# mLSTM pairs with two sum tiles and their own order, weight preparation placed behind the HGRN level copies, Silu written as Sigmoid and a product

## The chip, the cores and the metric

The kernel runs on one core of a Trainium2 chip. The metric is the device time of one execution in microseconds (us). A core has five engines, each with its own in-order queue: TensorE (PE, matmuls; PEld is the load of its weights, which runs beside it), VectorE (DVE), ScalarE (ACT), GpSimd (POOL) and SyncE (SP), which here only issues DMAs.

## What is computed

One step of a hybrid streaming encoder for 512 prompt frames and 32 sample frames (544 columns), all in float32 with a width of 1024. One wide projection feeds two branches: four mLSTM heads (matrix memory, width 512 a head) and eight HGRN2 heads (gated linear attention, width 128 a head). Two sigmoid gates merge the branches, and an output product and a gated per-layer embedding follow.

```python
xn = _rmsnorm(h, norm_g[l])
proj = xn @ w_in[l]
u, v_m, z_m, ig_pre, fg_pre, q_h, f_h, i_h, g_h, ga, gb = jnp.split(proj, ...)
c, conv_new = _causal_conv(u, conv0[l], conv_w[l], conv_b[l])
c = jax.nn.silu(c)
qm = einsum('bthd,hde->bhte', ch, w_qm[l])
km = einsum('bthd,hde->bhte', ch, w_km[l]) * (M_HD ** -0.5)
hm, C_new, n_new, m_new = _mlstm(qm, km, vm, ig, lf, C0, n0, m0)
hm = (_head_layernorm(hm, mnorm_g[l]) + m_skip[l] * c) * jax.nn.silu(z_m)
ya = hm @ w_brm[l]
lfh = jnp.log(lb + (1.0 - lb) * jax.nn.sigmoid(f_lin))
kh = (1.0 - lb) * jax.nn.sigmoid(-f_lin)
qh = jax.nn.silu(q_h)
oh, S_new = _hgrn(qh, kh, i_h, lfh, S0)
oh = _head_rmsnorm(oh, hnorm_g[l]) * jax.nn.silu(g_h)
yb = oh @ w_brh[l]
y = jax.nn.sigmoid(ga) * ya + jax.nn.sigmoid(gb) * yb
h = h + y @ w_out[l]
h = h + jax.nn.sigmoid(h @ w_pg[l]) * (p[l] @ w_ple[l])
out = _rmsnorm(h, final_g)
```

## The kernel before

**Precision.** A float32 operand is split in two parts, a high one (`...h`, a cast, mostly by ACT) and the low rest (`...l`, a subtraction, mostly by DVE). A product is three matmuls (high·high, low·high, high·low) that accumulate in PSUM. All 544 columns go in two halves of 272, each in its own PSUM half; a tile d, q, k, ya or yb is such a pair of halves.

**Pairs.** The projection `proj` is computed two units of 128 rows at a time. A `Two` takes units a and b and saves one product in eight by Strassen's scheme, in seven blocks of 12 matmuls: `a11`, `a12` and `a22` use a raw piece of the weights; `s1`, `s2`, `s3` and `s4` use sums of raw pieces. `form` makes the sums in the tiles `ws` (pool tag `wu`, `NSUM` of them) and splits them into `wsNh` and `wsNl` (`waNNh`, `waNNl` for raw pieces; the number behind is the unit: ws26 is the s2 of unit 6). The sums s1, s2 and s4 are made one over the other in one tile: s2 adds to s1, s4 adds to s2. `s3`, `s2` and `a22` write the same PSUM half, and between them ACT copies that half out (`t`, line 490), so a block in that half waits for the copy of the one before.

**Two kinds of pairs.** In the HGRN part and at the end pairs are `early` (the raw pieces are summed by accumulating DMAs that POOL issues, line 451 among them) or `apart` (the first of them, unit 48, which stands in the last mLSTM head). The mLSTM pairs (u, v and z) are neither, and their sums are DVE additions.

**The pump.** `Pump` lines the blocks of all pairs up in one order by the numbers in `PAIR`, and hands them out a half block at a time as filling between matmuls of the recurrences that wait for ACT and DVE. The order on PE is written by hand (`manual_schedule`). The orders on ACT and DVE come from a scheduler that takes instructions by readiness and priority; `high_priority` puts an instruction ahead, `issue_after(x)` keeps it from standing before x on x's engine. `pump.behind` is such an x for all weight preparations.

**The order of the work.** A first stretch (to about 60 us) takes the norm and the u pairs. Then four mLSTM heads: products k and q, scores (`sc`, line 844), `kt`, `vt` and `C`, then `nm` and `Cs`, then the transposes `yt`, then `ya`. In the first head the gate rows (lines 690 to 715, the generator `gates`) stand on DVE too: additions and scans over a 4 x 544 tile. The copies `z<-d` (line 653) empty the PSUM halves which k then takes. From 627 us eight HGRN heads of about 33.5 us each run: in each, seven levels (`LEVELS`) in which ACT copies `km` (line 1471), PE makes `pl` from it (line 1479), and DVE multiplies and selects (lines 1501, 1508). ACT makes the gates of the next head with Sigmoid (1388, 1389), its query with Silu (1397, 1398), and its output gate with Silu (1419). Then two sets of transposes `ht` (1546, copied to `kit` by ACT in 1550) and the state's product `su`. From about 935 us the last pairs (ga and gb, the merge gates) are computed, then `yb`, `o`, `pg` and the rest. The embedding p comes in by DMA as tiles p (line 1645) and is split to ps0 and ps1; `pleo` (line 1654) empties its product.

Of the kernel before, what the change touches and what calls it, by code (L numbers as in the profile page):

```python
# [14 lines left out]
ALU = mybir.AluOpType  # L15
# [27 lines left out]
NSUM = 4  # L43
# [10 lines left out]
GATED = 2  # L54
# [10 lines left out]
def hybrid_step(ctx: ExitStack, tc: tile.TileContext, a, o):  # L65
# [320 lines left out]
    class Two:  # L386
# [7 lines left out]

        def raws(self):
            a, b = self.unit, self.other
            return [(a, 0), (a, 1)] + ([] if self.early else [(b, 0)]) + [(b, 1)]
# [27 lines left out]
        def make(self, *forms):  # L425
            def go(raw):
                for form in forms:
                    if form not in self.w:
                        self.form(form, raw)

            return go

        def form(self, form, raw):
# [14 lines left out]
            src = raw[plain_[form]] if form in plain_ else q["s3" if form == "s3" else "s1"]  # L448
            self.w[form] = split_piece(src, f"w{form}{a}")
# [89 lines left out]
    ALONE, PAIR = (0, 1, 2, 3), (0, 1, 5, 4, 6, 9, 10)  # L539

    class Pump:


        def __init__(self, todo):
            self.done, self.when, self.behind, self.limit = 0, {}, None, None
            order, base = [], 0
            for n, e in enumerate(todo):
                if isinstance(e, One):
# [7 lines left out]
            self.begins = [(first.index((n, 0)) - LEAD, e) for n, e in enumerate(todo) if isinstance(e, Two) and e.early]  # L556
            self.order = [b for *_, b in sorted(order, key=lambda x: x[:3])]
# [7 lines left out]
        def prepare(self, upto):  # L565
            while self.made < min(upto, self.limit or len(self.order)):
# [72 lines left out]
    def fill(h):  # L639
# [9 lines left out]
        def gate_one(f, acc):  # L649
            z = eslot(f"z{h}{f}")  # L650
            for b in range(2):
                with tc.high_priority():
                    V.tensor_copy(z[:, b * TH : (b + 1) * TH], acc[b][:, :TH])
# [153 lines left out]
    def stage_q(h, u):  # L807
# [4 lines left out]
        w = t.pop("wq", None) or weight(a["w_qm"][h, u], f"wq{h}{u}")  # L812
# [89 lines left out]
    def mchain(h, pump):  # L902
# [76 lines left out]
        yield pump.clear(4)  # L979
# [188 lines left out]
    with tc.manual_schedule(engines={mybir.EngineType.Activation, mybir.EngineType.DVE, mybir.EngineType.PE}):  # L1168
# [145 lines left out]
        for _ in range(GATED):  # L1314
            next(gates)
    with tc.manual_schedule(engines={mybir.EngineType.PE}):
        for h in range(MH):
            if h:
                stage_decay(h)
            else:  # L1320
                st8[0].update(vt=vt, cc=cc, cs=cs)
                pump.to(EARLY)
            stage_k(h)
# [17 lines left out]
            if h == 0:  # L1341
                with tc.issue_after(low.ins):
# [29 lines left out]
    gbs, yas = [None] * KD, [None] * KD  # L1372

    def units():
# [19 lines left out]
        def query(h, qq):  # L1394
            tf, kk, kq = (hs[h][k] for k in ("tf", "kk", "kq"))
            q0 = eslot(f"q0{h}")
            S.activation(unrev(q0), qq[:, :HB], AF.Silu)
            S.activation(q0[:, HB:T], qq[:, HB:T], AF.Silu)
# [15 lines left out]
        def gate(h, t):  # L1414
            S.activation(t[:, :T], t[:, :T], AF.Silu)
            hs[h]["gg"] = t

        def merge_a(f, t):
# [3 lines left out]
            V.tensor_tensor(y, y, t[:, :T], ALU.mult)  # L1422
# [33 lines left out]
    def chain(h):  # L1456
# [9 lines left out]
        for li, c in enumerate(LEVELS):  # L1466
            smp = c < NS
            n = HB if smp else NA
            km = tp.tile([P, NA], F32, tag="vs", name=f"km{h}{c}", bufs=1)
            with tc.high_priority():  # L1470
                S.copy(  # L1471
                    km.rearrange("p (n j c) -> p n j c", j=2, c=c),
                    view(kk, HB, ((2 * c, NA // (2 * c)), (c - HB, 2), (1, c))),
                )
            yield STEPS[li]
# [66 lines left out]
        for n, src, dst, dss in ((0, ii, it, its), (1, kk, kt, kts)):  # L1542
# [15 lines left out]
        yield 3  # L1558
# [66 lines left out]
    obf = []  # L1625
# [17 lines left out]
    for k in range(2):  # L1643
        t = slot(f"p{k}")
        nc.sync.dma_start(t[:, :T], a["pT"][k])
        ps_.append(split(t[:, :T], f"ps{k}"))

    def ple_units(n):
        for f in range(len(ple), len(ple) + n):
# [3 lines left out]
            for b in range(2):  # L1653
                S.copy(t[:, half(b)], acc[b])
# [177 lines left out]
```

## Time and profile before

| quantity | value |
|---|---|
| median of 3 runs | 1186.71 us (1183.53 to 1187.61) |
| profiled execution | 1184.37 us |
| its span | 1182.7 us |
| POOL busy | 186.7 us (16%) |
| DMA moved | 159.93 MB, mean 135 GB/s |

The span is the part of the execution between the first and the last recorded instruction; 1.7 us of the profiled execution lie outside. An engine is busy when an instruction of it runs. A wait is put down to the instruction that ended it. A row of the timeline gives start, duration, engine, line, what is written and what is read; in square brackets at its end stands how long the engine had been idle and what it waited for. Line numbers are those of the kernel before, in the changed kernel they lie up to some 30 lines further on.

### The profile page before, as it was taken

The page shows a single profiled execution, that of the slowest core. Times are in us where ns is not written, and L with a number is a line of the kernel's source. Part 1 is how long each engine was busy: PE and PEld are TensorE (multiplying, and loading weights), DVE is VectorE, ACT ScalarE, POOL GpSimd, SP SyncE. Part 2 cuts the span into 40 slices and gives each one's busy share as a digit, 9 for nine tenths or more (in the row PEclk, how much of TensorE's full clock was granted, in tenths as well). Part 3 has the DMA queues.
Part 4 walks back from the last instruction along what each step waited for, and adds up shares of the span by engine and source line. Part 5 has one row for each costly group of instructions (what it writes and reads, how often), then busy time and mean ns, then how long its engine had stood idle before and what let it go on. Part 6 is the DMA issues. An engine that isn't in the chain of part 4 may idle for free.

```text
span 1182.7 us, 24120 instructions
## 1 busy us (share of the span) xinstructions
PE 1146.8 (97%) x8897; PEld 1117.9 (95%) x8897; DVE 885.4 (75%) x1975; ACT 701.1 (59%) x1521; POOL 186.7 (16%) x364
## 2 busy tenths in 40 slices
PE   9989999999999999999999999999999989999998
PEld 8989999999999999899989999999999989999998
DVE  6976988576886777976885688888888755654485
ACT  5666656656556565565654577777776655432462
POOL 4933010100001100001100122322222220000000
PEclk9999999999999999999999999999999989999999
DMA  6224215322353223542738666655666685432653
GB/s 227 64 90 129 75 46 163 119 95 95 126 168 127 90 91 128 156 158 78 229 101 261 159 137 135 135 126 127 133 155 131 165 226 130 147 95 81 232 170 112
DMA packets 91150, 159.93 MB, mean 135 GB/s; under 512 B 10260, under 2 KB 17812, under 8 KB 91032
## 3 DMA queue, kind: packets, MB, share of 16 engines
q1 hardware_dynamic: 80928, 140.24, 37.2%
q0 software_dynamic: 9936, 18.09, 9.6%
q8 instruction: 70, 1.15, 0.4%
q14 instruction: 48, 0.39, 0.1%
q10 hardware_dynamic: 168, 0.06, 0.0%
HBM read 133.44 MB, written 24.91 MB: 134 GB/s over the span
## 4 chain that ended last, share of the span: by engine, by line
PE 80%; DVE 9%; ACT 5%; DMA 4%; issue 3%; SPq 0%; POOL 0%; ACTq 0%; DVEq 0%; POOLq 0%
PE d L476 31%; PE ya L151 8%; PE pg L1691 4%; PE yb L151 4%; PE o L151 4%; PE k L151 4%; PE q L151 4%; PE C L884 4%; PE pl L1479 2%; PE nm L1058 2%; PE sc L844 2%; DMA ws<-in_w_in 2%; PE d L369 1%; DVE cv L618 1%; PE ple L151 1%
## 5 line engine op out<-in xcount | busy, mean ns | idle before, releaser
L405 POOL DMA_DIRECT2D ws<-in_w_in x46 | 40.4, 877 | 163.5 <-DMA ws<-in_w_in 36.8
L490 ACT COPY t<-d 128x272 f32<-128x272 f32 x126 | 47.4, 378 | 19.3 <-PE d L476 16.9
L1501 DVE TENSOR_TENSOR hkq<-hkq,q 128x288 f32<-128x288 f32 (+1 forms) x96 | 40.8, 432 | 16.3 <-PE pl L1479 12.6
L1479 PE MATMUL pl<-hkq,km 128*128 128x128 f32 x224 | 39.4, 298 | 4.5 <-ACT km L1471 4.4
L618 DVE SCALAR_TENSOR_TENSOR cv<-ub,vec,cv 128x547 f32<-128x547 f32 x48 | 40.3, 842 | 1.9 <-ACT cv L613 1.5
L1479 PEld LDWEIGHTS pl<-hkq,km 128*128 128x128 f32 x224 | 30.9, 189 | 7.7 <-ACT km L1471 6.4
L1471 ACT COPY km<-hkq 128x256 f32<-128x256 f32 x56 | 23.9, 427 | 16.2 <-PE d L476 12.3
L451 POOL DMA_DIRECT2D ws<-in_w_in x23 | 23.7, 1031 | 60.6 <-DVE ws272l L131 26.1
L988 DVE SCALAR_TENSOR_TENSOR c<-c,wi,Cs 128x258 f32<-128x258 f32 x32 | 15.1, 478 | 17.0 <-PE Cs L986 16.9
L1452 POOL TENSOR_SCALAR_AFFINE_SELECT aa<-at 128x128 f32<-128x128 f32 x32 | 20.7, 678 | 43.1 <-DVE at L1508 38.4
L1126 DVE TENSOR_TENSOR y<-ya,y 128x272 f32<-128x272 f32 x48 | 19.2, 436 | 9.9 <-PE ya L151 8.7
L1508 DVE COPY_PREDICATED at<-lmask,pl 128x288 f32<-128x288 uint8 (+1 forms) x56 | 26.3, 470 | 0.0
L896 ACT COPY Co<-C 128x258 f32<-128x258 f32 x32 | 10.4, 378 | 25.2 <-PE C L884 11.0
L782 POOL COPY vsm<-vt 128x96 f32<-128x96 f32 x16 | 6.4, 408 | 91.5 <-DVE vt L497 54.7
L1069 ACT COPY y<-nm 128x516 f32<-128x516 f32 x16 | 9.4, 589 | 17.6 <-PE nm L1058 17.5
L1598 ACT ACTIVATE osq<-kq 128x128 f32<-128x128 f32 x32 | 9.8, 305 | 15.2 <-DVE kq L1592 15.0
L858 ACT CAST sh<-dm 128x512 fp32r<-128x512 f32 (+3 forms) x16 | 7.4, 460 | 19.1 <-DVE dm L852 19.1
L1018 DVE BATCH_NORM_STATS2 bs<-y 128x6 f32<-128x512 f32 (+1 forms) x20 | 13.8, 691 | 6.1 <-ACT y L1069 6.0
L1058 PE MATMUL nm<-vhl,sh 128*128 128x258 f32 x112 | 18.3, 286 | 0.0
L960 POOL CAST vhl<-one 128x4 fp32r<-128x4 f32 x8 | 2.7, 340 | 98.1 <-PE nm L1058 98.1
L1678 DVE TENSOR_TENSOR h<-o,h 128x272 f32<-128x272 f32 x16 | 6.3, 437 | 14.5 <-PE o L151 14.5
L1665 DVE TENSOR_TENSOR gb<-yb,gb 128x272 f32<-128x272 f32 x16 | 6.3, 437 | 14.4 <-PE yb L151 14.4
(4485 smaller groups left out, 5094.8 us busy)
## 6 DMA issues: line engine op xcount, KB each, us to landing
ws<-in_w_in POOLq DMA_DIRECT2D x69, 256.0 KB, 4.8
ws<-in_w_in SPq DMA_DIRECT2D x46, 256.0 KB, 3.2
ya_d<-y SPq DMA_DIRECT2D x32, 272.0 KB, 2.2
y<-ya_d SPq DMA_DIRECT2D x24, 272.0 KB, 4.0
c<-in_C SPq DMA_DIRECT2D x16, 258.0 KB, 4.2
out_Cp<-Co SPq DMA_DIRECT2D x16, 258.0 KB, 2.7
out_Cs<-c SPq DMA_DIRECT2D x16, 258.0 KB, 2.7
x<-in_xT SPq DMA_DIRECT2D x8, 272.5 KB, 4.6
```

The source lines that it names most:

```text
L151: PE.matmul(both[b][:m, :TH], part(w, off + k * step, m, x), xx[:, half(b)], start=(k == 0 and j == 0), stop=(k == n - 1 and j == 2),)
L405: G.dma_start(t, w_in[u][:, i * WP : (i + 1) * WP], accum_op=ALU.add)
L476: PE.matmul(ps, ww[:, c], xx, start=(start and k == 0 and j == 0), stop=end, skip_group_check=not start,)
L490: S.copy(t, ps)
L618: V.scalar_tensor_tensor(cv[:, :547], ub[:, j : j + 547], vcol(V_CW + 4 * ft + j), cv[:, :547], ALU.mult, ALU.add)
L884: PE.matmul(pn[g][:, :VH], kw[b][x][:, f * P : (f + 1) * P], vv[b][y][:, g * VH : (g + 1) * VH], start=(b == 0 and j == 0), stop=(b == NB ...
L1058: PE.matmul(pn[:, g, :VH], st[j][x][:, (i - j) * P : (i - j + 1) * P], vv[j][y][:, g * VH : (g + 1) * VH], start=(j == 0 and q == 0), stop ...
L1471: S.copy(km.rearrange("p (n j c) -> p n j c", j=2, c=c), view(kk, HB, ((2 * c, NA // (2 * c)), (c - HB, 2), (1, c))),)
L1479: PE.matmul(pn[:, 0, b * P : (b + 1) * P], km[:, b * P : (b + 1) * P], view(qq, b * P, ((2 * c, P // (2 * c)), (HB + c, 2), (1, c))), star ...
L1501: V.tensor_tensor(x, x, d, ALU.mult)
L1508: V.copy_predicated(at[:, :n], lmask[:, li, :n], pn[:, 0, :n])
L1691: PE.matmul(ps, part(w, k * P, P, x), xx[:, c], start=(k == 0 and j == 0), stop=(k == KD - 1 and j == 2))
```

## The change

- `NSUM` is 5 instead of 4.
- A `Two` that is neither early nor apart no longer makes all sums in one tile: s1 has its own, and s2 and s4 share a second (s2 is s1 plus a piece, s4 is s2 plus a piece, by the same additions). Its blocks stand in the list in another order and are placed by `HEAD` (first of a list) or `NEXT` (behind another pair) instead of `PAIR`. For the last pair of a head (units 6, 10 and 14) PE's order of blocks was s2, s1, s3, a22, s4; now it is s2 (with s4 of the pair before and a12 behind it), s3, s1, a22, s4.
- Weight preparation of the `apart` pair (unit 48) has high priority. The last pair of the last list makes its s4 sum with a DVE addition instead of an accumulating DMA (`alone`).
- In the first head one step of `gates` fewer is taken ahead of the head, and it is taken after the z copies instead (`issue_after` the first copy). The second pieces of the first head's wq have high priority. Additions for pairs in that head stand behind `low` of the scores (`pump.pairs`).
- In HGRN, `pump.behind` is the latest `km` copy. Silu becomes Sigmoid and a product by its argument: the activations of lines 1397, 1398 and 1419 take Sigmoid, and DVE multiplies (sizes 288, 256 and 544 columns). The second `ht` and `su` stand at other steps of the chain (2 and 2 instead of 1 and 3).
- At the end p's DMA and split are bound behind the third last product of a merge gate (`gated[-3]`), and the copies `pleo` have high priority.

```diff
-NSUM = 4
+NSUM = 5
...
-GATED = 2
...
+            self.grows, self.alone = early or apart, False
...
+            if not self.grows:
+                return [
+                    (times[0], [(a, 0)], self.make("a11"), self.run("a11", 0, True, self.after1), []),
+                    (times[1], s1, self.make("s2"), self.run("s2", 0, False, self.after6), []),
+                    (times[2], [(a, 1)], self.make("a12"), self.run("a12", 1, True, self.after2), []),
+                    (times[3], [], self.make("s3"), self.run("s3", 0, False, self.after7), []),
+                    (times[4], [], self.make("s1"), self.run("s1", 1, True, self.after5), []),
+                    (times[5], [], self.make("a22"), self.run("a22", 0, False, self.after4), [k[1]]),
+                    (times[6], [], self.make("s4"), self.run("s4", 1, False, self.after3), [k[0]]),
+                ]
...
-                for form in forms:
-                    if form not in self.w:
-                        self.form(form, raw)
+                with tc.high_priority() if self.apart else nullcontext():
+                    for form in forms:
+                        if form not in self.w:
+                            self.form(form, raw)
...
-            if form == "s1" and not self.early:
+            if form == ("s1" if self.grows else "s2") and not self.early:
                 add(self.sum_tile("s1"), raw[b, 0], raw[b, 1])
             if form == "s2":
-                add(q["s1"], q["s1"], raw[a, 0])
+                q["s2"] = q["s4"] = q["s1"] if self.grows else self.sum_tile("s2")
+                add(q["s2"], q["s1"], raw[a, 0])
...
-            if form == "s2" and self.early:
-                G.dma_start(q["s1"], w_in[a][:, WP : 2 * WP], accum_op=ALU.add)
-            elif form == "s2":
-                add(q["s1"], q["s1"], raw[a, 1])
+            if self.early and form == "s2" and not self.alone:
+                G.dma_start(q["s4"], w_in[a][:, WP : 2 * WP], accum_op=ALU.add)
+            elif form == "s2" if self.grows else form in ("s2", "a12") and "s2" in self.w and "a12" in self.w:
+                add(q["s4"], q["s4"], raw[a, 1])
...
-    ALONE, PAIR = (0, 1, 2, 3), (0, 1, 5, 4, 6, 9, 10)
+    ALONE, HEAD, NEXT, PAIR = (0, 1, 2, 3), (0, 3, 1, 6, 5, 9, 11), (0, 3, 5, 6, 8, 9, 11), (0, 1, 5, 4, 6, 9, 10)
...
+                elif not e.grows:
+                    times, length = NEXT if isinstance(last, Two) else HEAD, 7
...
+            if todo[-1].__class__ is Two:
+                todo[-1].alone = True
...
-                    with tc.issue_after(self.behind.ins) if self.behind is not None else nullcontext():
+                    after = self.pairs if isinstance(self.todo[self.ids[self.made][0]], Two) and self.pairs else self.behind
+                    with tc.issue_after(after.ins) if after is not None else nullcontext():
...
-                    V.tensor_copy(z[:, b * TH : (b + 1) * TH], acc[b][:, :TH])
+                    out = V.tensor_copy(z[:, b * TH : (b + 1) * TH], acc[b][:, :TH])
+            st8[h].setdefault("copies", []).append(out)
...
-        w = t.pop("wq", None) or weight(a["w_qm"][h, u], f"wq{h}{u}")
+        with tc.high_priority() if u and not h else nullcontext():
+            w = t.pop("wq", None) or weight(a["w_qm"][h, u], f"wq{h}{u}")
...
-        for _ in range(GATED):
-            next(gates)
+        next(gates)
...
                 pump.to(EARLY)
+                with tc.issue_after(st8[0]["copies"][0].ins):
+                    next(gates)
...
+                pump.pairs = low
...
-            S.activation(unrev(q0), qq[:, :HB], AF.Silu)
-            S.activation(q0[:, HB:T], qq[:, HB:T], AF.Silu)
+            S.activation(unrev(q0), qq[:, :HB], AF.Sigmoid)
+            S.activation(q0[:, HB:T], qq[:, HB:T], AF.Sigmoid)
+            V.tensor_tensor(unrev(q0), unrev(q0), qq[:, :HB], ALU.mult)
+            V.tensor_tensor(q0[:, HB:T], q0[:, HB:T], qq[:, HB:T], ALU.mult)
...
-            S.activation(t[:, :T], t[:, :T], AF.Silu)
+            sg = slot(f"sg{h}")
+            S.activation(sg[:, :T], t[:, :T], AF.Sigmoid)
+            V.tensor_tensor(t[:, :T], t[:, :T], sg[:, :T], ALU.mult)
...
+            pump.behind = held[-1] if held else None
             with tc.high_priority():
-                S.copy(
+                low = S.copy(
...
+            held.append(low)
...
-        for n, src, dst, dss in ((0, ii, it, its), (1, kk, kt, kts)):
+        for n, src, dst, dss in ((0, ii, it, its), (2, kk, kt, kts)):
...
-        yield 3
+        yield 2
...
-        nc.sync.dma_start(t[:, :T], a["pT"][k])
-        ps_.append(split(t[:, :T], f"ps{k}"))
+        with tc.issue_after(gated[-3].ins):
+            nc.sync.dma_start(t[:, :T], a["pT"][k])
+            ps_.append(split(t[:, :T], f"ps{k}"))
...
-            for b in range(2):
-                S.copy(t[:, half(b)], acc[b])
+            with tc.high_priority():
+                for b in range(2):
+                    S.copy(t[:, half(b)], acc[b])
```

Three places show what moved. The first is DVE at the start of the first mLSTM head. `row` tiles are the gate rows; z is the tile that empties the PSUM halves; wi331l is the low part of a weight. Before:

```order
90 L131 TENSOR_TENSOR wi331l<-wi33r_897,wi331h 128x512
91 L694 SCALAR_TENSOR_TENSOR row_813<-fg,row_813 4x544
92 L698 SCALAR_TENSOR_TENSOR row_814<-rst,row_813 4x544
93 L699 SCALAR_TENSOR_TENSOR row_815<-ig,vec,row_814 4x544
94 L653 COPY z_1088<-d_1026 128x272
95 L653 COPY z_1088<-d_1027 128x272
96 L703 COPY d_822<-row_814 4x1 x3
```

Now, with the lines of the changed kernel:

```order
90 L130 TENSOR_TENSOR wi331l<-wi33r_897,wi331h 128x512
91 L667 COPY z_1064<-d_1002 128x272
92 L667 COPY z_1064<-d_1003 128x272
93 L709 SCALAR_TENSOR_TENSOR row_813<-fg,row_813 4x544
94 L713 SCALAR_TENSOR_TENSOR row_814<-rst,row_813 4x544
95 L714 SCALAR_TENSOR_TENSOR row_815<-ig,vec,row_814 4x544
96 L718 COPY d_822<-row_814 4x1 x3
```

The three row operations stand behind the two z copies instead of ahead of them; nothing else on DVE moves there.

The second place is PE at the end of the first mLSTM head, where the block a22 of unit 6 (wa226) begins. d_2386 (before) and d_2391 (now) are the PSUM half of s3 and a22, d_2392 is the other half. Before:

```order
1113 L476 MATMUL d_2386<-xfh_1808,ws36l 128x272
1114 L476 MATMUL d_2386<-xfh_1580,ws36h 128x272
1115 L476 MATMUL d_2386<-xfl_1581,ws36h 128x272
1116 L476 MATMUL d_2386<-xfh_1580,ws36l 128x272
1117 L476 MATMUL d_2386<-xfh_1562,wa226h 128x272
```

Now:

```order
1104 L483 MATMUL d_2391<-xfh_1580,ws36l 128x272
1105 L483 MATMUL d_2392<-xfh_1562,ws16h 128x272
...
1115 L483 MATMUL d_2392<-xfl_1581,ws16h 128x272
1116 L483 MATMUL d_2392<-xfh_1580,ws16l 128x272
1117 L483 MATMUL d_2391<-xfh_1562,wa226h 128x272
```

Before, a22 followed s3 directly in the same PSUM half; now the twelve matmuls of s1, in the other half, stand between.

The third place is ACT in the first HGRN head, around the copy km of level 32 (km_9445 before, km_9467 now). Before:

```order
817 L1388 ACTIVATE tf_9420<-kq_9170 128x288
818 L1388 ACTIVATE hkq_9169<-kq_9170 128x288
819 L1390 ACTIVATE tf_9420<-tf_9420,lb,lc 128x544
820 L1391 ACTIVATE hkq_9169<-hkq_9169,lc 128x544
821 L1397 ACT_TABLE_LOAD
822 L1397 ACTIVATE q_9454<-hkq_9169 128x288
823 L1471 COPY km_9445<-hkq_8616 128x256
```

Now:

```order
815 L1406 ACTIVATE tf_9442<-kq_9190 128x288
816 L1406 ACTIVATE hkq_9189<-kq_9190 128x288
817 L1408 ACTIVATE tf_9442<-tf_9442,lb,lc 128x544
818 L1409 ACTIVATE hkq_9189<-hkq_9189,lc 128x544
819 L1416 ACTIVATE q_9476<-hkq_9189 128x288
820 L1495 COPY km_9467<-hkq_8634 128x256
```

The load of another activation table is gone from this place. In the whole HGRN part sixteen of the seventeen loads at lines 1389, 1397 and 1419 are gone, and PE runs the same matmuls in another order.

More of the change, by code (lines that the diff above doesn't have):

```diff
@@ L536, in pair @@
         )
-    ALONE, PAIR = (0, 1, 2, 3), (0, 1, 5, 4, 6, 9, 10)
+    ALONE, HEAD, NEXT, PAIR = (0, 1, 2, 3), (0, 3, 1, 6, 5, 9, 11), (0, 3, 5, 6, 8, 9, 11), (0, 1, 5, 4, 6, 9, 10)
     class Pump:
         def __init__(self, todo):
-            self.done, self.when, self.behind, self.limit = 0, {}, None, None
+            self.done, self.when, self.behind, self.pairs, self.limit, self.todo = 0, {}, None, None, None, todo
             order, base = [], 0
             for n, e in enumerate(todo):
+                last = todo[n - 1] if n else None
                 if isinstance(e, One):
                     times, length = ALONE, 4
+                elif not e.grows:
+                    times, length = NEXT if isinstance(last, Two) else HEAD, 7
                 else:
@@ L978, in mchain @@
                     xf[k] = xf_sums(k)
-        yield pump.clear(4)
+        yield 4
         olds = [old(0), old(1)]
@@ L1623, in finish @@
         hs[h].clear()
-    obf = []
+    obf, held = [], []
     with tc.manual_schedule(engines={mybir.EngineType.PE}):
```

10 lines of the change are left out of this document (3 added, 7 removed).

## The prediction

> **What bounds the kernel now.** The page comes first: the busy shares by engine, and the clock granted to PE in 40 slices.
>
> ```profile
> PE 1146.8 (97%) x8897; PEld 1117.9 (95%) x8897; DVE 885.4 (75%) x1975; ACT 701.1 (59%) x1521; POOL 186.7 (16%) x364
> ...
> PEclk9999999999999999999999999999999989999999
> ```
>
> PE is busy for 1146.8 of 1182.7 us, so the kernel is bound by PE, and the change leaves PE's work alone: the same matmuls in another order. Only two things can go: the 35.9 us in which PE is idle, and the time lost where its clock is cut. The waits of PE, summed by releaser (total us, times, longest), name most of the first:
>
> ```profile
> PE d L476 <- ACT t L490: 9.5, 6, 3.5
> PE pl L1479 <- ACT km L1471: 4.4, 8, 1.5
> PE k L151 <- DVE z L653: 4.1, 1, 4.1
> PE d L476 <- DVE ws348l L131: 1.8, 1, 1.8
> PE vt L951 <- DVE vhl L959: 1.4, 2, 0.9
> PE yb L151 <- ACT pleo L1654: 1.2, 1, 1.2
> ...
> PE ht L1546 <- ACT kit L1550: 1.1, 6, 0.2
> ...
> PE d L476 <- DVE ws26l L131: 0.9, 1, 0.9
> ...
> PE q L151 <- DVE wq010l L131: 0.6, 1, 0.6
> ...
> PE d L476 <- ACT ws26h L130: 0.3, 1, 0.3
> ```
>
> The second is read from windows around the dips of the clock (start and end, length, PE busy, PEld, DVE, ACT, POOL, granted clock, DMA):
>
> ```profile
> 77.00:80.60 3.60, 3.05 (x13) 2.99 (x14) 3.53 (x13) 2.59 (x6) 0.52 (x1) 0.53 0.05 18
> 97.40:101.20 3.80, 3.80 (x21) 3.80 (x20) 2.54 (x9) 0.90 (x3) 2.47 (x6) 0.55 0.47 138
> 617.00:620.00 3.00, 1.18 (x9) 0.96 (x8) 2.91 (x6) 1.31 (x3) 0.00 (x0) 0.98 0.00 0
> 620.00:627.00 7.00, 6.19 (x29) 5.87 (x28) 4.70 (x8) 4.78 (x10) 1.74 (x2) 0.52 0.74 180
> ...
> 961.30:968.10 6.80, 5.80 (x26) 5.80 (x27) 3.93 (x7) 3.02 (x7) 0.00 (x0) 0.51 0.97 220
> ...
> 999.00:1002.20 3.20, 2.90 (x13) 2.90 (x14) 1.45 (x4) 0.86 (x4) 0.00 (x0) 0.51 0.33 95
> ...
> 1010.00:1183.00 173.00, 168.80 (x1344) 168.01 (x1344) 101.05 (x214) 69.52 (x140) 0.00 (x0) 1.00 0.42 136
> ```
>
> In five stretches the clock is about half. Length times one minus clock is what each costs: 1.7, 1.7, 3.4, 3.3 and 1.6, together 11.7 us. The third, for one, follows a stretch of little PE work (617 to 620: 1.18 us busy of 3). The last row is the end from 1010 us: 173 us at full clock, idle for 4.2, nearly all of it the tail behind the last matmul. The change has nothing to win there.
>
> **A. First head.** The timeline around the 4.1 us wait:
>
> ```profile
> 71.39 0.69 DVE L131 TENSOR_TENSOR wi331l<-wi33r,wi331h 128x512 fp32r<-128x512 f32 x1 [1.47 <-ACT wi331h L130]
> ...
> 73.36 0.71 DVE L694 SCALAR_TENSOR_TENSOR row<-fg,row 4x544 f32<-4x544 f32 x1 [1.28 <-ACT row L692]
> ...
> 73.91 1.28 POOL L131 TENSOR_TENSOR wk010l<-wk01r,wk010h 128x512 fp32r<-128x512 f32 x1 [2.83 <-ACT wk010h L130]
> 74.10 2.23 DVE L698 TENSOR_TENSOR_SCAN row<-rst,row 4x544 f32<-4x544 f32 x1
> ...
> 76.37 0.77 DVE L699 SCALAR_TENSOR_TENSOR row<-ig,vec,row 4x544 f32<-4x544 f32 x1
> 77.07 0.77 DVE L653 COPY z<-d 128x272 f32<-128x272 f32 x2
> ...
> 77.55 0.94 PE L151 MATMUL k<-cs0h,wk000h 128*128 128x272 f32 x2 [4.12 <-DVE z L653]
> ```
>
> k needs the PSUM halves that the z copies empty. With the three row operations behind them, the copies start when wi331l ends (72.08) and are done at 72.85, ahead of the end of the k block that runs until 73.4. So the 4.1 us go, and with them the idle that leads to the first dip (1.7). What is late next: PE is 4 us earlier, and the second k products need kf copies of the first pair (their PSUM) and wk011l. The z copies free the DVE late enough that the row chain, ACT's exponentials and its Silu stand in the same few us; POOL needs 1.28 for a low part. I take 1.3 us of new waits, between 0 and 2.6 (two POOL pieces). The wq010l wait (0.6) goes with the priority. The second dip (1.7) follows it only partly, since the stretch ahead of it also holds a row of tiny transposes: half of it, 0.85. A: −4.1 −1.7 −0.6 −0.85 +1.3 = **−6.0**.
>
> **B. Sums of the first head behind the scores.** Four DVE additions leave the stretch in which the first head's vhl is late (vhl 0.9 at the longest). I take **−0.5**, between −0.9, the whole wait, and +0.9, the same wait where the additions land, since DVE has work there too.
>
> **C. Order of the mLSTM pairs.** At the end of a head:
>
> ```profile
> 183.74 0.39 PE L476 MATMUL d<-xfh,wa226h 128*128 128x272 f32 x1 [0.91 <-ACT t L490]
> ```
>
> a22 follows s3 in the same PSUM half, so it pays the copy of t: 0.91. The block begins late as well, for the weights of s2, whose sum is made over the one before it in a single tile: 0.3 for ws26h, 0.9 for ws26l. Now twelve matmuls in the other half (1.5 us) stand between, more than the 0.91, and s2 has its own tile. 2.1 us a head at three heads: **−6.3**. Against it: s2 weights and two more products are formed in a new order, and in the heads after the first one casts have to keep up with the kt, vt and vts products. Nothing in the order puts one behind its use; I price a late one as the ws26l row (0.9), up to three, for the range.
>
> **D. The apart pair.** Its last wait but one:
>
> ```profile
> 622.24 0.60 PE L476 MATMUL d<-xfh,wa2248h 128*128 128x272 f32 x1 [0.81 <-ACT t L490]
> ```
>
> With priority, ws348l is formed right after ws248l, before the c and hm chain which held it: the 1.8 goes. So does the 7 us at 0.52 behind it (3.4). The 0.8 between s3 and a22 of this pair stays, its order is unchanged. Behind the priority hm15l now follows the copy-add of s4, which ends when ya starts; ya needs hm15l only as its last quarter, some 2.5 us later, and two DVE pieces of 0.7 fit. I add 0.3, up to 2. D: **−4.9**.
>
> **E. HGRN heads.** Around level 32 of the first head (ACT), then a later head (ACT and PE), the period (all engines), and the DVE product that prices the new ones (count, busy, mean ns, idle):
>
> ```profile
> 681.47 0.74 ACT L1391 ACTIVATE hkq<-hkq,lc 128x544 f32<-128x544 f32 x1
> 682.22 1.28 ACT L1397 ACT_TABLE_LOAD   x1
> ...
> 683.87 0.39 ACT L1471 COPY km<-hkq 128x256 f32<-128x256 f32 x1
> ...
> 713.80 0.38 PE L1479 MATMUL pl<-hkq,km 128*128 128x128 f32 x1 [0.42 <-ACT km L1471]
> ...
> 695.00:728.50 33.50, 32.90 (x257) 31.30 (x256) 29.18 (x78) 24.23 (x60) 9.24 (x14) 1.00 0.63 140
> L1399 DVE TENSOR_TENSOR hkq<-q,tf 128x544 f32<-128x544 f32 x8 | 5.8, 721 | 2.7 <-ACT q L1398 2.7
> ```
>
> PE is idle 0.6 us a head, and 1.47 once. Without the load km starts 1.28 earlier, and as the weight casts stand behind the km copies the rest goes too. Gone: 1.4 + 2.9 (seven times 0.42) + 1.1 (the six kit waits) = 5.4. ACT loses two loads a head, 2.6 us. DVE gains two times 0.72 = 1.4 us a head (544 columns of query in two parts, 544 of gate) and goes from 29.2 to 30.6 of a period that shrinks to 32.9. It has 2.3 us left, but its work for the levels stands in one queue with these products, and any product standing ahead of it delays it by up to 0.7. I take 0.3 us a head as new, eight times: +2.4, between 0 and 8 × 1.4 = 11.5. E: −5.4 + 2.4 = **−3.0**.
>
> **F. Last pairs.** SP, ACT and PE:
>
> ```profile
> 948.34 0.33 SPq L120 DMA_DIRECT2D wi94r<-in_w_in  x1
> 952.12 0.33 SPq L404 DMA_DIRECT2D ws<-in_w_in  x1
> ...
> 952.99 0.42 SPq L1645 DMA_DIRECT2D p<-in_pT  x1
> ...
> 958.24 0.65 ACT L103 CAST ps0h<-p 128x544 fp32r<-128x544 f32 x1 [3.42 <-DMA p<-in_pT]
> ...
> 997.79 0.62 ACT L130 CAST ws494h<-ws 128x512 fp32r<-128x512 f32 x1 [3.19 <-DMA ws<-in_w_in]
> ...
> 999.30 0.60 PE L476 MATMUL d<-xfh,ws394h 128*128 128x272 f32 x1 [2.48 <-ACT t L490]
> ```
>
> ACT stands 3.4 us for p, with the t copies behind it, and PE waits 3.5 for those. SP issues nothing from 948.7 to 952.1: its next DMA fills a sum tile, and the four are in use. p comes right behind. A fifth tile frees SP earlier; a p issued 3.5 us earlier is there when ACT asks, and the wait (3.5) and its dip (3.3) go. Later ACT stands 3.2 us for the accumulated sum of s4; a DVE addition from pieces that are loaded takes 0.7 instead, so PE's 2.5 and the last dip (1.6) go. The pleo wait (1.2) goes with the priority. ps1 is bound later now, and a Sigmoid stands ahead of the t copy: +0.9 for both, between 0 and 3.4 (a second wait for p like the first). F: −3.5 −3.3 −2.5 −1.6 −1.2 +0.9 = **−11.2**.
>
> **The sum.** −6.0 −0.5 −6.3 −4.9 −3.0 −11.2 = −31.9 from the profiled 1184.4: 1152.5. The median of the runs lies 2.3 above the profiled execution, of which I carry half a microsecond: **1153**. With none of the new waits (1.3 + 0.85 + 0.3 + 2.4 + 0.9 = 5.75) it is 1147, the low end.
>
> [...] The idle of 1.8 us at 617.44 in the trace was followed by 7 us at 0.52. [...]
>
> **Rivals.**
> - *Dips stay.* The clock at 620 and 999 (3.4 + 1.6) is cut for another reason than these waits: 1158. For: the gaps are short. Against: both dips directly follow such a gap. Chance 0.05.
> - *p still late.* The fifth sum tile is taken up by earlier loads and SP stands just as long; ACT's order of ps0h is the same as before. The 3.5 and 3.3 of F stay: 1160. For: SP issues in order, and five tiles are one more pair's look-ahead. Chance 0.18.
> - *The orders don't do what they say.* In the mLSTM heads the pair blocks wait for weights formed later instead of for t; C is 0 (1159) or pays three times 0.9 (1162). For: DVE is full in these stretches. Chance 0.12.
> - *DVE becomes the bound in HGRN.* The products delay the level chain by 1.4 a head: 11.5 instead of 2.4: 1162. Chance 0.10.
> - *Slower than before.* [...] Chance 0.04, and 0.03 that it ends about equal.
>
> My forecast has the rest, 0.48; two of the rivals together give up to 1169. The range is 1146 to 1169. What a measurement can tell from no change is 0.3%, 3.6 us: faster 0.93, same 0.03, slower 0.04, as only the last rival reaches the other side.
>
> **What would show it.** In the changed profile: no wait of k for z and z right behind wi331l (A); waits of d for t down from 9.5 to about 1 us, all of it the apart pair (C, D); no table load between the km copies, the km wait near 0, DVE about 30.6 of a head, heads of 32.9 to 33.2 us (E); ps0h without a DMA wait (F); granted clock 1.00 but for the start. I am wrong if PE busy plus idle moves elsewhere: a new wait over 1 us in the heads, or a clock of 0.5 in HGRN.

## The result and the profile after

| | before | after |
|---|---|---|
| median | 1187.16 us (1183.53 to 1187.67, 4 runs) | 1148.34 us (1147.13 to 1148.86, 4 runs) |
| ratio, 95% interval | | 0.9678 (0.9657 to 0.9699) |
| profiled execution, span | 1184.37, 1182.7 us | 1147.83, 1146.0 us |

The kernel is 3.2% faster. From span to span 36.6 us are gone. The same two rows of the page, after:

```profile
PE 1132.1 (99%) x8897; PEld 1109.6 (97%) x8897; DVE 894.1 (78%) x2000; ACT 677.4 (59%) x1505; POOL 198.8 (17%) x363
...
PEclk9999999999999999999999999999999999999999
```

PE's idle time went from 35.9 to 13.9 us, which is 22 of the 36.6. The other 14.7 us left PE's *busy* time, though it ran the same 8897 matmuls. Some 8.7 of them are clock: PE's busy time in the five stretches at about half clock, times one minus the clock, was 10.4 us before, and 1.7 is left. (The 11.7 of the prediction took the whole length of the stretches, in which PE is also idle at times.) Some 6 us more are neither idle nor clock; the section on the prediction finds them. The waits of PE (total, times, longest), after:

```profile
PE d L483 <- ACT t L497: 3.7, 2, 2.8
PE warm L1190 <- DVE emc L1028: 1.1, 1, 1.1
PE Cs L1002 <- DVE c L1004: 0.9, 3, 0.5
PE vt L967 <- DVE vhl L975: 0.9, 1, 0.9
PE pl L1504 <- ACT km L1495: 0.6, 1, 0.6
PE k L150 <- POOL wk011l L130: 0.6, 1, 0.6
PE k L150 <- ACT kf L810: 0.3, 1, 0.3
```

Of 9.5 us behind t copies 3.7 are left, of 4.4 behind km 0.6, and the waits for z, ws348l, pleo, kit, ws26l and wq010l are gone from the list. New are two short ones in the first head's k. Windows of the changed kernel, columns as before (granted clock is the third from the end):

```profile
60.00:80.00 20.00, 19.43 (x149) 18.60 (x147) 16.84 (x25) 16.20 (x30) 7.32 (x5) 1.00 0.32 106
80.00:103.00 23.00, 22.55 (x173) 21.67 (x174) 14.90 (x41) 17.78 (x48) 7.60 (x26) 1.00 0.45 143
600.00:627.00 27.00, 25.82 (x202) 25.13 (x200) 20.70 (x47) 13.63 (x27) 1.22 (x2) 1.00 0.80 241
...
927.00:932.10 5.10, 2.30 (x18) 2.07 (x17) 2.27 (x4) 3.96 (x8) 2.63 (x3) 1.00 0.87 160
932.10:935.60 3.50, 3.50 (x17) 3.50 (x17) 1.26 (x3) 1.52 (x3) 0.00 (x0) 0.51 0.89 208
```

Both dips of the first head, the one in the apart pair and the one near 1000 us are gone. One is left, at 932, behind 2.8 us of idle.

Where the time went, by the start of the same matmul in both traces:

| from the start to | before | after | gained in this part | predicted |
|---|---|---|---|---|
| first sc (A) | 104.07 | 98.26 | 5.8 | 6.0 |
| first yt (B) | 167.11 | 160.25 | 1.1 | 0.5 |
| ya of heads 1, 2, 3 (C) | 186.87, 339.25, 492.07 | 177.38, 327.64, 477.97 | 2.6, 2.1, 2.5 | 6.3 in all |
| ya of head 4 (D) | 627.33 | 608.41 | 4.8 | 4.9 |
| wa1190, the last pairs (E) | 938.26 | 908.47 | 10.9 | 3.0 |
| end of the span (F) | 1182.7 | 1146.0 | 6.8 | 11.2 |

Parts A to D came out nearly as summed. E gave three and a half times its term and F three fifths of it; the experiments go there first.

### The profile page after: what moved, and what is told of

It reads as the page before. It is cut to its first block, busy times and chain, and to the rows that moved or that the text cites. A ratio compares the mean times of both kernels' runs of the same rounds, so it can differ in the third digit from the quotient of the medians.

```text
span 1146.0 us, 24132 instructions
## 1 busy us (share of the span) xinstructions
PE 1132.1 (99%) x8897; PEld 1109.6 (97%) x8897; DVE 894.1 (78%) x2000; ACT 677.4 (59%) x1505; POOL 198.8 (17%) x363
## 4 chain that ended last, share of the span: by engine, by line
PE 88%; DVE 6%; ACT 3%; DMA 1%; issue 1%; POOL 0%; SPq 0%; ACTq 0%; DVEq 0%
PE d L483 37%; PE ya L150 8%; PE pg L1718 4%; PE q L150 4%; PE yb L150 4%; PE o L150 4%; PE C L900 4%; PE k L150 4%; PE sc L860 3%; PE pl L1504 2%; PE nm L1074 2%; PE d L368 1%; PE ple L150 1%; DVE cv L632 1%; PE nm L1051 1%
## 5 line engine op out<-in xcount | busy, mean ns | idle before, releaser
L1504 PE MATMUL pl<-hkq,km 128*128 128x128 f32 x224 | 36.9, 287 | 0.7 <-ACT km L1495 0.6
L1475 POOL TENSOR_SCALAR_AFFINE_SELECT aa<-at 128x128 f32<-128x128 f32 x32 | 25.1, 819 | 27.6 <-DVE at L1533 23.8
L912 ACT COPY Co<-C 128x258 f32<-128x258 f32 x32 | 10.4, 378 | 29.1 <-PE C L900 24.7
L624 POOL COPY uo<-ub 128x3 f32<-128x3 f32 x16 | 16.3, 1016 | 39.3 <-DVE ub L506 29.2
L797 POOL COPY ksm<-kf 128x96 f32<-128x96 f32 x16 | 7.2, 450 | 57.9 <-ACT kf L810 57.9
```

What stands on the lines that cost most here:

```text
L1504: PE.matmul(pn[:, 0, b * P : (b + 1) * P], km[:, b * P : (b + 1) * P], view(qq, b * P, ((2 * c, P // (2 * c)), (HB + c, 2), (1, c))), star ...
```

## The experiments

Every kernel is the changed one with the edit shown. The time of the kernel before, taken anew beside each set, came out with medians of 1183.5 to 1187.2, so differences of less than about 3 us between sets are left to the traces.

The first HGRN head differs between the kernels for a reason that no edit aims at. In the profiled executions of four of them (a22 behind s3, the apart pair, ht, p late) ACT stands 3.1 to 3.5 us there for a sum by an accumulating DMA (1.0 in the changed kernel). PE then waits 2.7 to 3.1 us for km (0.6 in the changed kernel), and the clock is cut behind it (p late: 0.59 from 657.4 to 661.0 us and 0.94 to 665.0; ht: 0.71 from 658.3 to 662.0 and 0.84 to 666.0; each worth 3.4 us at half clock), some 3.5 us in that head together. So parts and heads are compared, and not only totals.

### Silu back

```diff
-            S.activation(unrev(q0), qq[:, :HB], AF.Sigmoid)
-            S.activation(q0[:, HB:T], qq[:, HB:T], AF.Sigmoid)
-            V.tensor_tensor(unrev(q0), unrev(q0), qq[:, :HB], ALU.mult)
-            V.tensor_tensor(q0[:, HB:T], q0[:, HB:T], qq[:, HB:T], ALU.mult)
+            S.activation(unrev(q0), qq[:, :HB], AF.Silu)
+            S.activation(q0[:, HB:T], qq[:, HB:T], AF.Silu)
...
-            sg = slot(f"sg{h}")
-            S.activation(sg[:, :T], t[:, :T], AF.Sigmoid)
-            V.tensor_tensor(t[:, :T], t[:, :T], sg[:, :T], ALU.mult)
+            S.activation(t[:, :T], t[:, :T], AF.Silu)
```

> The changed kernel with Silu back in HGRN (query and output gate): two table loads a head return on ACT (16 in all, 1.28 us each in the trace of before) and 1.4 us of products a head leave DVE. Theory (the loads made km and kit late, and each wait of PE costs more than the idle that the trace shows, about 0.27 us more each): a head goes from 32.1 us back towards 32.9 to 33.3, the kernel is 6 to 10 us slower than the changed one (1154 to 1158). Rival (binding the weight casts behind km was enough, the loads stood in ACT's idle time): within 1.5 us of the changed kernel. Second rival (the products on DVE cost as much as the loads): faster than the changed kernel by 1 to 3 us.

Measured: 1154.82 us (1153.43 to 1156.15), ratio 0.9747 (0.9724 to 0.9769). The loads matter, as the theory had it, and the heads take 32.55 us instead of 32.09, less than the forecast 32.9 to 33.3. Remarkably, the list of PE's waits names none in these later heads. Level 32 of a head, PE, in this kernel:

```profile
759.49 0.29 PE L483 MATMUL d<-xh,ws452l 128*128 128x272 f32 x1
759.81 0.61 PE L1500 MATMUL pl<-hkq,km 128*128 128x128 f32 x3
```

pl starts 0.32 us behind the last matmul of the filling, where the dense pace is 0.13. The last filling matmul is recorded as 0.29 long, so all but 0.03 of the 0.19 us of waiting fall under its tail, and no row of waits names them. Laid matmul by matmul against the changed kernel, a head falls behind by 0.29 here and by 0.18 at the pl of two earlier levels, which together is the 0.46.

### The binding behind km taken away

```diff
-            pump.behind = held[-1] if held else None
+            pump.behind = None
```

> The changed kernel without the binding of weight preparations behind the km copies in HGRN; Sigmoid stays. Theory (the loads were most of it, the binding the rest): one km wait a head returns, 0.4 us of idle and about 0.27 of restart at eight heads, 4 to 6 us slower than the changed kernel (1152 to 1154). Rival (without loads ACT is early enough that a cast ahead of km does no harm): within 1 us.

Measured: 1147.96 us (1147.52 to 1148.09), no change, and heads of 32.09 us: the rival. Without table loads ACT is early enough for a cast ahead of km.

### Both undone

The two edits above together.

> The changed kernel with Silu back in HGRN and the weight preparations unbound, both undone together. Alone, Silu back cost 0.45 us a head and unbinding nothing. Theory (they are two remedies for one wait, km behind a table load and a cast on ACT): together they cost more than the sum, 0.8 to 1.0 a head (heads of 32.9 to 33.1 us), 8 to 10 us slower than the changed kernel (1156 to 1158). Rival (they add): heads of 32.55 us as with Silu alone, 1153 to 1156.

Measured: 1156.34 us (1153.89 to 1159.62), heads of 33.08 us, as the theory had it: alone the edits cost 0.46 and 0 a head, together 0.99. The change had two remedies for one wait: Sigmoid alone removes all of it, the binding alone about half. The old waits are back, in the list of PE's waits:

```profile
PE pl L1500 <- ACT km L1491: 4.4, 8, 1.5
```

These are 0.42 us of shown idle a head, and they cost 0.99.

### ht and su at their old steps

```diff
-        for n, src, dst, dss in ((0, ii, it, its), (2, kk, kt, kts)):
+        for n, src, dst, dss in ((0, ii, it, its), (1, kk, kt, kts)):
...
-        yield 2
+        yield 3
```

> The changed kernel with the second transposes ht and the product su of an HGRN head at their old steps. Theory (the old place made PE wait for kit): a wait of 0.2 and a restart of about 0.27 return at seven or eight heads, 3 to 4 us slower (1151 to 1152). Rival (kit was late only because ACT stood in table loads): within 1 us.

Measured: 1150.69 us (1150.0 to 1155.35), heads of 32.47 us, 0.38 more than after: the theory, and this wait doesn't need the table loads. PE at the second ht:

```profile
771.43 0.28 PE L483 MATMUL d<-xh,wa1153l 128*128 128x272 f32 x1
771.90 0.66 PE L1571 MATMUL ht<-ident,hkq 128*128 128x128 f32 x4 [0.19 <-ACT kit L1575]
```

0.19 of shown idle cost 0.38. The 0.99 of the last run and this 0.38 make 1.37, all but 0.02 of the 1.39 us that a head gained.

### More work on DVE

```diff
             V.tensor_tensor(t[:, :T], t[:, :T], sg[:, :T], ALU.mult)
+            for _ in range(2):
+                V.tensor_copy(sg[:, :T], t[:, :T])
```

> The changed kernel with two more copies of 128 x 544 on DVE in each HGRN head behind the product of the output gate (work that changes no result). Theory (DVE has slack there, and products that stand ahead of the level chain delay it only if they come in its way): under 3 us slower than the changed kernel. Rival (DVE is at its limit in HGRN, so each us of DVE work costs one us): eight heads with the duration of two copies, 0.6 to 1.4 a head, 5 to 11 us slower.

Measured: 1175.68 us (1173.86 to 1179.44), 27 us slower for 16 copies of 0.44 us, 7 us of work in all. Both theories missed it. The waits of PE in this kernel, a window of 270 us in its HGRN part, and DVE and PE at the end of a head's norm:

```profile
PE hoT L1643 <- DVE kq L1629: 15.7, 7, 2.6
```

```profile
660.00:930.00 270.00, 254.24 (x1909) 244.34 (x1909) 224.48 (x601) 165.16 (x432) 62.42 (x97) 0.95 0.56 129
```

```profile
681.75 0.16 DVE L1627 TENSOR_SCALAR hv<-hv 128x5 f32<-128x5 f32 x1
...
694.53 0.74 DVE L1629 TENSOR_TENSOR kq<-kq,hr 128x512 f32<-128x512 f32 x1
...
695.42 0.41 PE L1643 MATMUL hoT<-anti,kq 128*128 128x128 f32 x2 [2.17 <-DVE kq L1629]
```

hoT, the transposes of a head's normalised output, now wait for DVE, 2.2 to 2.6 us in each of seven heads. In DVE's queue the norm is a chain of twelve small operations of 0.16 us, from hv on (a reciprocal root by iteration), which the scheduler puts one by one between large weight products; the copies drew the chain apart. 15.7 us are the waits, and some 13 the clock: 0.95 over 254 us of PE's work. The same chain and hoT in the changed kernel:

```profile
682.81 0.16 DVE L1625 TENSOR_SCALAR hv<-hv 128x5 f32<-128x5 f32 x1
...
692.39 0.68 DVE L1627 TENSOR_TENSOR kq<-kq,hr 128x512 f32<-128x512 f32 x1
...
694.15 0.27 PE L1641 MATMUL hoT<-anti,kq 128*128 128x128 f32 x1
```

and in the kernel before:

```profile
736.59 0.16 DVE L1600 TENSOR_SCALAR hv<-hv 128x5 f32<-128x5 f32 x1
...
743.65 0.69 DVE L1602 TENSOR_TENSOR kq<-kq,hr 128x512 f32<-128x512 f32 x1
...
748.82 0.27 PE L1616 MATMUL hoT<-anti,kq 128*128 128x128 f32 x1
```

From hv to the end of kq the chain takes 7.8 us before, 10.3 after and 13.5 with the copies: 0.9 us of added work made it 3.3 longer. From the end of kq to hoT there were 4.5 us before, and 1.1 are left after. So the change used 3.4 us of this slack, 2.5 of them by the longer chain, and it ends 1.1 us short of a cliff that the busy time of DVE (29.6 of 32.1 us a head) doesn't show:

```profile
715.00:747.10 32.10, 32.10 (x257) 31.11 (x256) 29.59 (x82) 21.72 (x60) 9.46 (x13) 1.00 0.62 137
```

### a22 behind s3 again

```diff
-    ALONE, HEAD, NEXT, PAIR = (0, 1, 2, 3), (0, 3, 1, 6, 5, 9, 11), (0, 3, 5, 6, 8, 9, 11), (0, 1, 5, 4, 6, 9, 10)
+    ALONE, HEAD, NEXT, PAIR = (0, 1, 2, 3), (0, 3, 1, 6, 5, 9, 11), (0, 3, 5, 8, 6, 9, 11), (0, 1, 5, 4, 6, 9, 10)
```

> The changed kernel with s1 ahead of s3 again in the mLSTM pairs that follow a pair, so that a22 follows s3 in the same PSUM half; the sum tiles stay two. Theory (a22 pays the copy of t): the waits of 0.9 us and a restart of about 0.27 return at every pair of that kind whose filling stands alone, three ends of heads: 3 to 4 us slower (1151 to 1153), with idle of 0.9 at wa226, wa2210 and wa2214. Rival (the sum tiles were the gain, and a free t copy comes in time): no change within 1 us.

Measured: 1176.44 us (1174.52 to 1177.24), 28 us slower. The theory was right in kind and far too small. The waits of PE in this kernel:

```profile
PE d L483 <- ACT t L497: 16.3, 15, 3.2
PE d L483 <- DVE z L504: 4.3, 6, 0.9
...
PE d L483 <- DVE ub L504: 2.7, 3, 1.1
PE d L483 <- DVE vt L504: 1.6, 3, 0.6
```

26 of the 29 us between the two spans lie in the mLSTM part, the rest mainly in the first HGRN head's wait. With this table every pair behind another pays, not three: a22 waits for the t copy of s3, and s1, now behind a12 in the other half, for DVE's addition that empties it (the 12 waits for z, ub and vt, 8.6 us). Before, the blocks of other pairs stood between most of them. In this run a block right behind another in the same PSUM half cost about 0.9 of idle each time behind ACT's copy and 0.7 behind DVE's addition, and the table decides how often.

### Four sum tiles

```diff
-NSUM = 5
+NSUM = 4
```

> The changed kernel with four sum tiles. Theory (the fifth tile is what lets the mLSTM pairs hold two sums and still load ahead): waits of PE for casts of ws return in the mLSTM heads, and SP stands longer for a free tile: 3 to 8 us slower than the changed kernel (1151 to 1156). Rival (the fifth tile did not free SP ahead of p, and the pairs' order hides the rest): within 1.5 us.

Measured: 1150.62 us (1146.96 to 1152.17), between both. The trace has waits of 0.42 us each for the s2 weights of units 10 and 14, and, in the last pairs, 1.9 at wa2286 and 0.7 at ws394, which the changed kernel hasn't. The wait at ws384 is 3.5 instead of 2.8. By the medians the fifth tile is worth some 2 us, less than the theory had, and the runs alone can't tell that from nothing. In the traces most of it lies at the end: the last pairs take 3.4 us longer.

### The apart pair without priority

```diff
-                with tc.high_priority() if self.apart else nullcontext():
+                with nullcontext():
```

> The changed kernel without the high priority of the apart pair's weights (unit 48). Theory (the priority alone moved ws348l ahead of the c and hm chain): the wait of about 1.8 at ws348l and the half clock behind it return, 3.5 to 5.5 us slower (1152 to 1154). Rival (the other moves already brought it forward, or the clock isn't cut by 1.8 us of idle): under 2 us slower, or the wait without the half clock.

Measured: 1152.81 us (1148.67 to 1153.67), the time that the theory gave. The wait is 3.7 us instead of 1.8, though, and stands at ws248l now, two blocks earlier; behind it follows a window at 0.62:

```profile
603.00:606.80 3.80, 3.50 (x18) 3.51 (x18) 3.80 (x7) 2.17 (x4) 0.00 (x0) 0.62 0.21 71
```

From the third ya to the fourth it takes 5.1 us longer than the changed kernel. The first HGRN head's wait and the missing wait at ws384 cancel behind it.

### The gate rows ahead of z again

```diff
-        next(gates)
+        next(gates)
+        next(gates)
...
-                with tc.issue_after(st8[0]["copies"][0].ins):
-                    next(gates)
```

> The changed kernel with the gates step of the first head taken ahead of the z copies again. Theory (the row operations ahead of z were the whole 4.1 us wait and the half clock behind it; what is late next is 0.94 us of waits for kf and wk011l, which vanish again behind the longer wait): 4.1 + 0.3 + 1.7 - 1.4 = 4.5 to 6 us slower than the changed kernel (1153 to 1154), and a dip of the granted clock near 77 us. Rival (the other waits stay and the clock is not cut): 3 us or less.

Measured: 1152.06 us (1150.94 to 1155.56), with a span 4.7 us over that of the changed kernel. The wait of 4.12 us for z is back, both short waits of k are gone, and from 77 to 81 us the clock is 0.50: the theory, step by step. All of the difference lies ahead of the first sc (103.31 against 98.26).

### The end: p late, and sums by DVE

p's cast stands 3.7 us in ACT's queue in the changed kernel too, at the same place:

```profile
922.32 0.48 SPq L1671 DMA_DIRECT2D p<-in_pT  x1
...
927.81 0.65 ACT L102 CAST ps0h<-p 128x544 fp32r<-128x544 f32 x1 [3.71 <-DMA p<-in_pT]
...
931.87 0.39 PE L483 MATMUL d<-xfh,ws384h 128*128 128x272 f32 x1 [2.80 <-ACT t L497]
```

The change binds the product ps0l on DVE behind a merge gate, but the cast on ACT is bound to nothing. Three kernels vary this. First, the cast bound as well (`acts` holds the Sigmoids of merge_a):

```diff
-            S.activation(t[:, :T], t[:, :T], AF.Sigmoid)
+            acts.append(S.activation(t[:, :T], t[:, :T], AF.Sigmoid))
...
-        with tc.issue_after(gated[-3].ins):
+        with tc.issue_after(gated[-3].ins), tc.issue_after(acts[-3].ins):
```

> The changed kernel with ps0's cast bound on ACT behind the third last Sigmoid of a merge gate as well (its product on DVE is bound already), the DMA at the same place. Theory (ACT stood 3.7 us for p, with the t copy of ws384 behind it, and PE's 2.8 us and the half clock behind them come from that alone): both go, 2.8 + 1.7 + 0.3 of restart: 4 to 5 us faster than the changed kernel (1143 to 1144), granted clock 1.00 all through the end. Rival (what is behind ps0h waits for something else too, such as DMAs of sums): the gain is under 2 us, and another releaser stands at ws384.

Measured: 1146.45 us (1144.74 to 1151.06), the rival: the wait at ws384 is gone, and PE waits 1.95 us at wa2284 and 1.36 at wa2292 instead. In the profiled execution, the longest of the four, the last pairs are only 0.4 us shorter than in the changed kernel. ACT at the first of them:

```profile
937.92 0.62 ACT L129 CAST ws484h<-ws 128x512 fp32r<-128x512 f32 x1 [5.70 <-DMA ws<-in_w_in]
```

The next thing that ACT stands for is a sum by an accumulating DMA. Second, the s4 sums of four pairs by DVE, without the late cast:

```diff
-            if todo[-1].__class__ is Two:
-                todo[-1].alone = True
+            for e in todo[1:2] + todo[-4:]:
+                if isinstance(e, Two):
+                    e.alone = True
```

> The same additions without the late cast of p. Theory (p alone makes the 2.8 us wait at ws384 and the half clock): that wait stays, and with the first head's wait gone the gain is 0.5 to 1.5 us (1146.5 to 1148). Rival (the accumulating DMAs delay p's own by holding the sum tiles, so that SP is late): the wait at ws384 goes as well, 1143 to 1145.

Measured: 1144.81 us (1144.12 to 1148.01). The theory's mechanism, at a time in the rival's range: the wait at ws384 stays (2.1 us) and the first HGRN head's wait for km is gone. The gain is larger than forecast mainly because no half clock (1.7 us) followed the wait this time (granted clock 1.00, rows in the last section). Third, both edits:

> Both at the end: ps0's cast bound late on ACT as in the run before, and the s4 sums of the pairs 49, 92, 84 and 86 made by a DVE addition instead of an accumulating DMA. Theory (with p out of the way ACT stood 5.7 us for an accumulated sum, which is a DMA behind another one in POOL's queue): the waits at wa2284 and wa2292 go and the first HGRN head loses its wait for km: 1142 to 1144, and the spread of single runs falls. Rival (SP and the sum tiles are the bound at the end, so the next piece is late): 1145 or more, with a wait for another weight.

Measured: 1142.68 us (1141.97 to 1144.79), ratio 0.9657 (0.9640 to 0.9674), as the theory had it. In the last pairs PE has no wait left (110 us, granted clock 1.00):

```profile
900.00:1010.00 110.00, 110.00 (x871) 108.88 (x870) 75.79 (x142) 61.03 (x125) 8.20 (x10) 1.00 0.57 157
```

It is the fastest kernel of the study: its slowest run is below the fastest of the changed kernel (1147.13), though the intervals of their two ratios overlap.

## Why the prediction was right, and where its sizes were off

1148.3 lies in the range (1146 to 1169), in the direction forecast. The mechanisms of A, C and D came out as told, and E's too, except for what a wait costs. The forecast of 1153 was 4.7 too high, mainly the sum of two errors of opposite sign, 7.9 in E and 4.4 in F; that they cancel in part is luck.

- **A, first head:** 5.8 for 6.0. The z copies start right behind wi331l, as read from the order; the new waits are 0.35 for kf and 0.59 for wk011l, the two named, 0.9 for the 1.3 taken:

```profile
72.03 0.69 DVE L130 TENSOR_TENSOR wi331l<-wi33r,wi331h 128x512 fp32r<-128x512 f32 x1 [1.48 <-ACT wi331h L129]
72.64 0.78 DVE L667 COPY z<-d 128x272 f32<-128x272 f32 x2
...
77.42 0.68 PE L150 MATMUL k<-cs0h,wk010h 128*128 128x272 f32 x2 [0.35 <-ACT kf L810]
...
80.45 0.39 PE L150 MATMUL k<-cs2h,wk011l 128*128 128x272 f32 x1 [0.59 <-POOL wk011l L130]
```

  The dip at 97 went whole, of which half was counted. Ahead of it PE shows only 0.6 us of idle in 3.4, beside a row of tiny transposes; what set it off was not tried.
- **B:** 1.1 for 0.5; which of the waits it came from was not tried by itself.
- **C, pairs' order:** 7.2 for 6.3. wa226 now starts 0.12 us behind the last matmul of the block ahead of it, the dense pace:

```profile
174.24 0.29 PE L483 MATMUL d<-xfh,ws16l 128*128 128x272 f32 x1
174.36 0.29 PE L483 MATMUL d<-xfh,wa226h 128*128 128x272 f32 x1
```

  No weights of s2 are late. The rival "the orders don't do what they say" is out.
- **D, apart pair:** 4.8 for 4.9, the wait and its clock. The 0.9 between s3 and a22 stayed as said. The run without priority bears out both, as far as the clock hangs on the wait.
- **E, HGRN heads:** the term that was mis-sized, 10.9 for 3.0. That the loads, the order behind km and the place of ht cause the waits is borne out by the runs above; two steps of the sum were wrong. First, "= 5.4" took the waits at their shown idle. The idle time did fall by 5.2, but PE's busy time fell by 5.6 more, for the same matmuls at full clock. This part before and after:

```profile
627.33:938.26 310.93, 304.76 (x2365) 291.64 (x2364) 252.49 (x651) 210.75 (x507) 71.57 (x105) 1.00 0.64 151
608.41:908.47 300.06, 299.11 (x2365) 290.61 (x2364) 260.46 (x677) 190.73 (x495) 79.65 (x105) 1.00 0.65 156
```

  Level 32 of a head shows where it went. PE before:

```profile
713.09 0.29 PE L476 MATMUL d<-xh,ws450l 128*128 128x272 f32 x1
713.80 0.72 PE L1479 MATMUL pl<-hkq,km 128*128 128x128 f32 x4 [0.42 <-ACT km L1471]
```

  and after:

```profile
692.60 0.29 PE L483 MATMUL d<-xh,ws450l 128*128 128x272 f32 x1
692.72 0.61 PE L1504 MATMUL pl<-hkq,km 128*128 128x128 f32 x4
```

  From start to start 0.71 us passed before and 0.12 after, 0.59 more, while the row shows 0.42: the record of a matmul is 0.29 long at a pace of 0.13, so about the first 0.16 us of a wait count as busy. The four pl then took 0.72 instead of 0.61, since the first one behind a wait is followed after 0.22 instead of 0.11. So this wait cost 0.69, which is what is shown plus 0.27, and a wait under 0.16 isn't shown at all. Laid matmul by matmul against the changed kernel, a later head of the kernel before falls behind by 0.69 here and by 0.40 at the second ht (shown: 0.42 and 0.19), and by 0.30 at the pl of three other levels, where nothing is shown. That is 1.39 a head instead of the 0.60 that the rows show; with 1.2 in the first head it makes the 10.9. Second, the 2.4 set aside for DVE products in the way of the chain were not needed: no wait of that kind came. Two of the signs were off with it: heads took 32.09 us instead of 32.9 to 33.2, and DVE is busy for 29.6 of a head instead of 30.6.
- **F, last pairs:** 6.8 for 11.2. The step that failed is "A fifth tile frees SP earlier; a p issued 3.5 us earlier is there when ACT asks". SP still stood from 918.9 to 921.4 (2.5 us, for 3.4 before), p came 5.5 us after its issue, and ACT stood 3.7. The rival "p still late", given 0.18, is what happened here: 2.8 of 3.5 us and one of the two dip windows stayed. The rest of F (s4 by DVE, pleo) came about as summed.
- **Clock:** four of five stretches went. For three of them the wait ahead went too, those of 1.8 and 2.5 us of idle included; the one at 97 had no wait of that size. The rival "dips stay" is out. The length of the idle alone does not decide it in the traces: 1.8 us in the kernel before was followed by half clock, and 2.1 us in the run with additions alone by a clock of 1.00.
- **The slower side:** the run with more DVE work shows where it lies: idle of 2.2 to 2.6 us in each of seven heads, and a granted clock of 0.95 over the 270 us around them. It does not lie in the level chain, but in the norm's small operations, and 0.9 us more DVE work a head took 27 of the 39 us gained.

## What to carry to other kernels

A wait of PE cost more here than its idle time shows (0.69 us for 0.42, 0.38 for 0.19); compare start to start against the dense pace, and count it by the number of waits. A binding holds on the engine of the instruction that it names, so a split over two engines needs one for each. And when work moves to an engine with free time, the slack that counts is that of its slowest chain of small operations (here 4.5 us that became 1.1), not the free share of its busy time.

## What was not expected of the hardware

The same idle didn't always cost clock. Three waits of PE that were followed by half clock are 1.82 us for ws348l in the kernel before (0.50 from 619.85 to 626.68 us), 2.48 for ws394h there (0.50 from 998.73 to 1002.14) and 2.80 for ws384h in the changed kernel (0.51 from 932.1 to 935.6). In the run with more DVE work a wait of 2.17 us ended at 695.42, and from 693.5 to 697 the clock was 0.82 on average (0.95 over the 270 us with all seven waits).

In the run with additions alone PE waited as long, 2.1 us at ws384, and the clock stayed full:

```profile
927.90:930.10 2.20, 0.10 (x2) 0.03 (x1) 1.38 (x4) 2.20 (x6) 0.87 (x1) 1.00 0.59 105
930.10:934.00 3.90, 3.90 (x31) 3.90 (x32) 2.64 (x5) 1.73 (x4) 0.00 (x0) 1.00 0.84 195
934.00:938.00 4.00, 4.00 (x35) 4.00 (x34) 2.99 (x6) 2.85 (x6) 0.87 (x1) 1.00 0.38 99
```

The run with both Silu and the binding undone had a wait of 2.9 us for a t copy, and the mean granted clock of that whole execution was 1.000. The other way round, in the kernel before half clock at 97 us (0.50 from 97.61 to 101.03) stood behind a stretch of 3.4 us in which PE was idle for only 0.64:

```profile
94.18:97.60 3.42, 2.78 (x31) 2.54 (x31) 1.97 (x6) 3.29 (x10) 1.07 (x3) 1.00 0.51 168
```

So in these runs the length of a wait alone doesn't tell whether clock is lost, and what tells the cases apart was not shown: no experiment moved a wait by itself. The stretches at 0.50 and 0.51 named here lasted 3.4 us or more, so each lost 1.7 us or more.
